# A two-layer hybrid trunk on one core: a reordered chain between sub-layers, and triangular inverses with compact blocks transposed on TensorE

## The chip, the core and the metric

The kernel runs on one core of a Trainium2 chip. Times are device microseconds (us) of that core. The engines are named as the profile names them: PE is TensorE (matmul; PEld is its weight load), DVE is VectorE, ACT is ScalarE, POOL is GpSimd, SP is SyncE, which issues the weight DMAs. Each engine works through its own instructions in order.

## The reference

Two layers, each a token mixer and then a convolutional feed-forward block. Around every one of the four sub-layers stands the same pattern: a modulated RMSNorm in front, a gated RMSNorm behind, and the residual add.

```python
for layer in range(DEPTH):
    mod_p = adaln(c_ctx[None, :], mod_w[layer], mod_b[layer])      # six vectors of 1024
    mod_s = adaln(c, mod_w[layer], mod_b[layer])
    hs = modulated_rmsnorm(xs, n_mix_pre[layer], mod_s[:, 0], mod_s[:, 1])
    ...                                                            # mixer of hp and hs gives op, os_
    xs = xs + mod_s[:, 2, None, :] * rmsnorm(os_, n_mix_post[layer])
    hs = modulated_rmsnorm(xs, n_ffn_pre[layer], mod_s[:, 3], mod_s[:, 4])
    xs = xs + mod_s[:, 5, None, :] * rmsnorm(conv_ffn(hs, *ffn[layer]), n_ffn_post[layer])
def modulated_rmsnorm(x, w, shift, scale):
    return rmsnorm(x, w) * (1.0 + scale[:, None, :]) + shift[:, None, :]
def gated_delta_scan(q, k, v, g, beta, s0):                        # chunks of 128, both directions
    ia = a_strict + jnp.eye(CHUNK)                                 # unit lower triangular, per head
    u = lax.linalg.triangular_solve(ia, vc * bc[..., None], left_side=True, lower=True)
    w = lax.linalg.triangular_solve(ia, kbeta * jnp.exp(gcs)[..., None], left_side=True, lower=True)
```

The prompt has 128 tokens and the sample 256; d_model is 1024 and the feed-forward width 2816. Layer 0 mixes with SSD heads and gated DeltaNet heads, layer 1 with spatial-gating MLP groups and windowed attention.

## The kernel before

All tokens lie side by side in T = 386 columns (128 prompt, 2 of gap, 256 sample), features on the 128 partitions, so the residual stream `xres` is 8 tiles of 128x386. Every dense product is made in three matmuls of split operands (weight high times input high, weight high times input low, weight low times input high): in `acc` (L378 to L380) tile by tile, and in `group` (L393, L395) k by k over up to three output tiles at once. A weight tile comes by one DMA into a `wst` buffer (`fetch`), is cast on ACT (`whi`, L345) and subtracted on DVE (`wlo`, L348). A Tile scheduler fixes the order on each engine by priorities and estimated costs; `tc.issue_after` adds an edge to it.

`Net.residual` is the chain between two sub-layers, run four times: gap 0 (mixer 0 to feed-forward 0), gap 1 (feed-forward 0 to mixer 1), gap 2 (mixer 1 to feed-forward 1), and the last. It needs the sums of squares of the sub-layer's output, of the gated output, and of gated output times x. Tiles 0 to 6 add theirs into `sums` on DVE and POOL (L520). In the middle of tile 7 the callback `before` puts the first of the sums through `colsum` on PE (L498, three 128x1 matmuls for each); behind tile 7 come the other sums and the parts of tile 7 (squares L526, L508; product L530). The root is an add on DVE (L409) and a power on POOL (L412); `spread` sends it back to all partitions on PE (L420); four short DVE instructions (L544 to L411) make the second root's argument. Then `update` forms u on DVE (L563) and adds it to x on POOL (L564), `prenorms` multiplies by the second root (L471), modulates on ACT (L473) in two segments (prompt, sample) and splits into `hh` (ACT, L371) and `hl` (DVE, L372), on which the next matmuls wait.

Beside this runs the adaLN work of the layer as side work in quads: `quads` loads four `wmod` tiles and runs 16 pairs of short matmuls in each of four steps (`pmod`, L301; the profile records a quad as 64), copies the result on ACT (L305), transposes it on PE (L308) and adds the bias on DVE (L310). `step(n)` advances it by n steps; S0, S1 and S2 say how many steps each gap takes behind the first spread, behind the second, and behind each k of `prenorms`; Q0 to Q5 say how many steps other stages take.

The DeltaNet heads need the inverse of a unit triangular 128x128 matrix for each of 8 heads, in 3 chunks. The inverse is built from blocks: 16x16 by scalar recursion on DVE (L887, L889), then 32, 64 and 128 wide by `square` on PE (L922 and L967 to L976). Two matrices PF and PB of 128x8x128 hold the blocks of both directions; the blocks needed as left operands are transposed on DVE (L944 into L2, 4 of 32x256 a chunk, and L962 into L3, 8 a chunk).

## Time and profile before

| what | value |
|---|---|
| median of 3 runs | 1449.47 us (1449.01 to 1450.84) |
| profiled execution, its own time | 1449.51 us |
| its span, mean granted clock of PE | 1447.7 us, 0.975 |
| PE busy | 1379.6 us, 95% of the span |
| DVE, ACT, POOL busy | 956.8, 792.7, 198.4 us |
| chain that ended last, PE's share | 79% |

The span is the time between the first and the last instruction of the profiled execution; its own time has 1.8 us more around it. The 40 slices of the page show PE at 8 or 9 tenths nearly everywhere, but these average over stages: where PE stands idle is read in the timeline around each gap and in the waits of the stretch with the inverses (140 to 262 us).

### The profile page before, as it was taken

What the parts mean: (1) busy time and instruction counts of PE and PEld (TensorE: products, weight loads), DVE (VectorE), ACT (ScalarE), POOL (GpSimd) and SP (SyncE); (2) the same over time, 40 slices, a digit from 0 to 9 for tenths busy, and PEclk for the clock granted to TensorE, in tenths of its full rate; (3) what the DMA queues carried; (4) which work ended last, traced back from release to release, by engine and by line L of the source; (5) the groups of instructions that cost most, each with busy time, mean ns of one, the idle gap of its engine ahead of it and who ended that gap; (6) DMA issues with size and microseconds to landing.
All of it is one profiled execution on the core that took longest, in us unless ns stands there. A gap on an engine that the chain in (4) does not pass through costs nothing.

```text
span 1447.7 us, 26153 instructions
## 1 busy us (share of the span) xinstructions
PE 1379.6 (95%) x10133; PEld 1306.4 (90%) x10133; DVE 956.8 (66%) x1879; ACT 792.7 (55%) x1749; POOL 198.4 (14%) x186
## 2 busy tenths in 40 slices
PE   5999998999998999999999999999999999999996
PEld 3889887999987789899999998999999899999996
DVE  3586999855989766676666445566567486767432
ACT  3578665668585436555455444544855465555341
POOL 0023110012355304200000113000002300000001
PEclk9999999999999999899999999999999999999998
DMA  9334544412643474545543442544234334343441
GB/s 347 130 101 142 174 138 143 142 42 79 199 161 117 139 238 170 210 154 162 170 134 114 128 126 74 160 146 134 83 117 153 125 117 131 117 131 115 128 126 55
DMA packets 60332, 201.58 MB, mean 139 GB/s; under 512 B 7120, under 2 KB 12000, under 8 KB 60208
## 3 DMA queue, kind: packets, MB, share of 16 engines
q1 hardware_dynamic: 52832, 186.25, 40.1%
q10 hardware_dynamic: 6048, 8.93, 1.7%
q0 software_dynamic: 1328, 4.73, 1.1%
q8 instruction: 80, 1.31, 0.4%
q14 instruction: 44, 0.36, 0.1%
HBM read 191.20 MB, written 8.68 MB: 138 GB/s over the span
## 4 chain that ended last, share of the span: by engine, by line
PE 79%; DVE 11%; issue 3%; ACT 3%; POOL 3%; DMA 1%; POOLq 0%; SPq 0%; ACTq 0%; DVEq 0%
PE mm L393 19%; PE mm L378 11%; PE mm L379 11%; PE mm L380 11%; PE mm L395 9%; PE pmod L301 3%; DVE wlo L348 2%; PE ps L498 1%; DVE t L700 1%; PE ps L1625 1%; PE mmt L1550 1%; PE mmt L1551 1%; PE mmt L1552 1%; DVE er L1133 1%; POOL er L809 1%
## 5 line engine op out<-in xcount | busy, mean ns | idle before, releaser
L348 DVE TENSOR_TENSOR wlo<-wst,whi 128x512 fp32r<-128x512 f32 (+1 forms) x497 | 344.2, 699 | 189.0 <-ACT whi L345 185.0
L345 ACT CAST whi<-wst 128x512 fp32r<-128x512 f32 (+1 forms) x505 | 304.2, 612 | 282.9 <-PE mm L379 151.2
L393 PE MATMUL mm<-hh,whi 128*128 128x386 f32 x728 | 247.7, 340 | 5.8 <-ACT hh L371 4.9
L393 PE MATMUL mm<-hh,wlo 128*128 128x386 f32 x728 | 245.9, 338 | 0.0
L395 PE MATMUL mm<-hl,whi 128*128 128x386 f32 x728 | 239.6, 340 | 0.3
L378 PE MATMUL mm<-hh,whi 128*128 128x386 f32 x552 | 198.0, 359 | 4.7 <-ACT t L1341 2.8
L380 PE MATMUL mm<-hh,wlo 128*128 128x386 f32 x552 | 191.6, 347 | 0.6 <-DVE wlo L348 0.6
L379 PE MATMUL mm<-hl,whi 128*128 128x386 f32 x552 | 191.9, 348 | 0.0
L393 PEld LDWEIGHTS mm<-hh,whi 128*128 128x128 f32 x728 | 137.1, 188 | 8.6 <-ACT hh L371 5.8
L395 PEld LDWEIGHTS mm<-hl,whi 128*128 128x128 f32 x728 | 136.1, 188 | 1.5 <-DVE hl L372 1.4
L393 PEld LDWEIGHTS mm<-hh,wlo 128*128 128x128 f32 x728 | 137.3, 189 | 0.0
L378 PE MATMUL mm<-gh,whi 128*128 128x386 f32 x352 | 119.5, 339 | 0.0
L379 PE MATMUL mm<-gl,whi 128*128 128x386 f32 x352 | 119.2, 339 | 0.0
L380 PE MATMUL mm<-gh,wlo 128*128 128x386 f32 x352 | 118.9, 338 | 0.0
L378 PEld LDWEIGHTS mm<-hh,whi 128*128 128x128 f32 x552 | 107.5, 195 | 11.9 <-issue 6.1
L598 DVE SCALAR_TENSOR_TENSOR t<-mm,vecs,t 128x385 f32<-128x385 f32 x88 | 54.3, 618 | 87.1 <-ACT t L597 87.1
L379 PEld LDWEIGHTS mm<-hl,whi 128*128 128x128 f32 x552 | 107.4, 195 | 0.7 <-issue 0.2
L380 PEld LDWEIGHTS mm<-hh,wlo 128*128 128x128 f32 x552 | 106.5, 193 | 1.0 <-DVE wlo L348 0.9
L700 DVE SCALAR_TENSOR_TENSOR t<-mm,vecs,t 128x384 f32<-128x384 f32 (+1 forms) x152 | 92.7, 613 | 12.3 <-ACT t L694 8.1
L597 ACT ACTIVATE t<-mm,vecs 128x386 f32<-128x386 f32 x88 | 58.9, 674 | 72.4 <-PE mm L395 72.4
L520 POOL TENSOR_TENSOR sums<-sums,t 128x386 f32<-128x386 f32 x36 | 41.5, 1175 | 337.6 <-DVE t L517 281.4
L301 PE MATMUL pmod<-wmod,cond 128*32 128x128 f32 x1536 | 67.2, 297 | 0.3 <-issue 0.3
(423 smaller groups left out, 2589.9 us busy)
## 6 DMA issues: line engine op xcount, KB each, us to landing
wmod<-modw_l SPq DMA_DIRECT2D x96, 512.0 KB, 4.4
wst<-up_l SPq DMA_DIRECT2D x88, 512.0 KB, 3.5
wst<-w SPq DMA_DIRECT2D x56, 512.0 KB, 4.0
wst<-wo SPq DMA_DIRECT2D x32, 512.0 KB, 3.9
wst<-down_l SPq DMA_DIRECT2D x32, 512.0 KB, 3.6
wst<-w1f SPq DMA_DIRECT2D x18, 512.0 KB, 3.6
wst<-down_l SPq DMA_DIRECT2D x16, 384.0 KB, 3.2
wst<-w1t SPq DMA_DIRECT2D x10, 512.0 KB, 3.6
```

What stands on the lines that cost most here:

```text
L301: nc.tensor.matmul(acc[32 * c:32 * c + 32, 0:128], self.cond[:, k, :], w[:, o:o + 128], start=(k == 0), stop=(k == 7), tile_position=(0, 3 ...
L345: self.conv_hi = nc.scalar.copy(out=hi[:, 0:m], in_=st[:, o:o + m])
L348: self.conv_lo = eng.tensor_sub(out=lo[:, 0:m], in0=st[:, o:o + m], in1=hi[:, 0:m].bitcast(F32))
L378: mm(ps, wh, xh, start=start, stop=False)
L379: mm(ps, wh, xl, start=False, stop=False)
L380: return mm(ps, wl, xh, start=False, stop=stop)
L393: mm(ps, w[k // 4][p][:, s], hh[:, k, :], start=(k == 0 and p == 0), stop=False)
L395: mm(ps, w[k // 4][0][:, s], hl[:, k, :], start=False, stop=(k == 7))
L520: (nc.gpsimd if i else v).tensor_add(out=acc[:, i, :], in0=acc[:, i, :], in1=p)
L597: nc.scalar.activation(out=cv, in_=ps, func=AF.Identity, scale=cw(1), bias=self.v(f"ffb_l{l}", n))
L598: stt(out=cv[:, 1:T], in0=ps[:, 0:T - 1], scalar=cw(0), in1=cv[:, 1:T], op0=ALU.mult, op1=ALU.add)
L700: nc.vector.scalar_tensor_tensor(out=o, in0=p, scalar=cw(i), in1=o, op0=ALU.mult, op1=ALU.add)
```

## The change

Three things are changed. In the chain between sub-layers the sums of tiles 0 to 6 (in gap 0 of tiles 0 to 5, with tile 6's parts summed on their own) are all taken inside the last tile; the callback comes at k = 14 instead of 16 in the feed-forward blocks, at 4 instead of 5 in mixer 0, and four k later in mixer 1; the third weight tile is fetched right behind the last tile, half of it converted there and half behind the first k of `prenorms`; the first add to x is made on DVE, and the sample segment of the first k is modulated on DVE. The steps of the adaLN work change place: every gap now takes four (one quad): one behind the last tile, and one between and two behind the two spreads, these three held behind the last `colsum`; before, the constants gave gaps 0, 1 and 2 10, 10 and 6 steps. A quad's copy on ACT now comes with the step behind its fourth. Q2, Q4 and Q5 rise, so that other stages take more. In the inverses PF's and PB's diagonal blocks are first made in compact tiles Pd (128x8x32), their transposes are matmuls with an identity on PE followed by copies on ACT, and Pd is copied into PF on ACT and into PB on POOL.

```diff
-S0, S1, S2 = [1, 2, 2], [9, 8, 4], [0, 0, 0]
+S0, S1, S2 = [1, 1, 1], [2, 2, 2], [1, 1, 1]
...
-            for k in (2 * j, 2 * j + 1):
...
-            if j == 3:
-                s = self.t386()[:, 0:128]
-                nc.scalar.copy(out=s, in_=acc[:, 0:128])
+            with self.follow(self.hold):
...
+                        nc.tensor.matmul(acc[32 * c:32 * c + 32, 0:128], self.cond[:, k, :], w[:, o:o + 128],
+                                         start=(k == 0), stop=(k == 7), tile_position=(0, 32 * c))
             yield 0.45
+        s = self.t386()[:, 0:128]
+        nc.scalar.copy(out=s, in_=acc[:, 0:128])
...
-    def fetch(self, after):
...
         st = self.wst.tile([128, 1024], F32, name="wst", tag="wst")
         nc.sync.dma_start(out=st[:, 0:n], in_=src)
         parts = []
+        self.ready.append((src, parts))
+        self.rest = self.halves(st, n, parts)
+        if halves:
+            next(self.rest)
+        else:
+            drain(self.rest)
+
+    def halves(self, st, n, parts):
+        nc = self.nc
         for o in range(0, n, 512):
             m = min(512, n - o)
             hi, lo = (self.spare(n) or p.tile([128, 512], F32R, name=n, tag=n) for n, p in (("whi", self.whi), ("wlo", self.wlo)))
-            with self.follow(after and after[0]):
-                self.conv_hi = nc.scalar.copy(out=hi[:, 0:m], in_=st[:, o:o + m])
+            self.conv_hi = nc.scalar.copy(out=hi[:, 0:m], in_=st[:, o:o + m])
             eng = nc.gpsimd if o and self.help else nc.vector
-            with self.follow(after and after[1]):
-                self.conv_lo = eng.tensor_sub(out=lo[:, 0:m], in0=st[:, o:o + m], in1=hi[:, 0:m].bitcast(F32))
+            self.conv_lo = eng.tensor_sub(out=lo[:, 0:m], in0=st[:, o:o + m], in1=hi[:, 0:m].bitcast(F32))
             parts.append((hi, lo))
-        self.ready.append((src, parts))
+            yield
...
             if update:
-                update(k)
-            nc.vector.tensor_mul(out=h, in0=self.x[:, k, :], in1=r)
+                with self.follow(first and k > 1 and first.ins):
+                    update(k)
+            with self.follow(first and first.ins):
+                nc.vector.tensor_mul(out=h, in0=self.x[:, k, :], in1=r)
             for s, (b, e) in enumerate(SEGS):
+                if update and k == 0 and s:
+                    first = nc.vector.tensor_scalar(out=h[:, b:e], in0=h[:, b:e], scalar1=a[:, k, s:s + 1],
+                                                    scalar2=m[:, k, 0, s:s + 1], op0=ALU.mult, op1=ALU.add)
+                    continue
                 nc.scalar.activation(out=h[:, b:e], in_=h[:, b:e], func=AF.Identity,
                                      scale=a[:, k, s:s + 1], bias=m[:, k, 0, s:s + 1])
-            self.split(hh[:, k, :], hl[:, k, :], h)
-            if update:
-                self.step(S2[self.gap])
+            cast, cut = self.split(hh[:, k, :], hl[:, k, :], h)
+            if update and k == 0:
+                with self.follow(cast.ins), self.follow(cut.ins):
+                    drain(self.rest)
...
+        direct = self.gap == 0
+
         def before():
-            colsum(0, acc[:, 0, :], True)
-            colsum(0, part[0], False)
+            for i in range(num):
+                colsum(i, acc[:, i, :], i == 0)
+            if direct:
+                colsum(0, part[0], False)
...
-            if n:
-                for i, p in list(enumerate(part))[n // 6:]:
+            if 0 < n < 7 - direct:
+                for i, p in enumerate(part):
                     (nc.gpsimd if i else v).tensor_add(out=acc[:, i, :], in0=acc[:, i, :], in1=p)
...
+        six = part
         o = out_tile(7, before)
+        if not last:
+            self.fetch(1)
+        if direct:
+            colsum(2, six[2], False)
...
             for b, e in SEGS:
                 ox = v.tensor_mul(out=part[2][:, b:e], in0=o[:, b:e], in1=gx[:, b:e])
-            colsum(2, acc[:, 2, :], True)
+            self.step(S0[self.gap])
         colsum(0, part[0], False)
...
         if not last:
-            colsum(1, acc[:, 1, :], True)
+            if direct:
+                colsum(1, six[1], False)
...
-            self.step(S0[self.gap])
+            self.hold = tail.ins
+            self.step(S2[self.gap])
             r2 = self.spread(rt2)
             self.step(S1[self.gap])
-            self.prefetch(3, (sq.ins, self.roots[0]))
+            self.hold = None
...
                 v.tensor_mul(out=u[:, n, :], in0=u[:, n, :], in1=r)
-                eng.tensor_add(out=self.x[:, n, :], in0=self.x[:, n, :], in1=u[:, n, :])
+                (eng if n else v).tensor_add(out=self.x[:, n, :], in0=self.x[:, n, :], in1=u[:, n, :])
...
-                    if mid and k0 + k == 16:
+                    if mid and k0 + k == 14:
                         mid()
...
-Q2 = 1
+Q2 = 2
 Q0 = 0
 Q3 = 8
-Q4 = 10
-Q5 = 15
+Q4 = 11
+Q5 = 21
...
-        L = self.w.tile([128, 8, 32], F32, name="L", tag="t2")
-        v.tensor_scalar_mul(out=L[:, :, 0:16], in0=col(TX, 0), scalar1=me)
-        v.tensor_scalar_mul(out=L[:, :, 16:32], in0=col(TXT, 24), scalar1=mo)
+        LP = self.w.tile([128, 2, 8, 32], F32, name="LP", tag="t2")
+        L = LP[:, 0]
+        nc.scalar.activation(out=L[:, :, 0:16], in_=col(TX, 0), func=AF.Copy, scale=me)
+        nc.scalar.activation(out=L[:, :, 16:32], in_=col(TXT, 24), func=AF.Copy, scale=mo)
         yield 0.0, 3.0
-        for a in range(4):
-            p = slice(32 * a, 32 * a + 32)
-            nc.gpsimd.tensor_tensor(out=PB[p, :, 32 * a:32 * a + 32].rearrange("p h (e c) -> p h e c", e=2),
...
-            for P, i, o in ((PF, TXT, 0),):
-                for e in range(2):
-                    nc.scalar.activation(out=P[p, :, 32 * a + 16 * e:32 * a + 16 * e + 16],
-                                         in_=i[p, :, 16 * e + o:16 * e + o + 8].rearrange("p c h -> p h c"),
-                                         func=AF.Copy, scale=(me, mo)[e][p])
+        Pd = self.w.tile([128, 8, 32], F32, name="Pd", tag="Pd"), LP[:, 1]
+        nc.gpsimd.tensor_tensor(out=Pd[1].rearrange("p h (e c) -> p h e c", e=2),
+                                in0=TX.rearrange("p c (e i) -> p i e c", e=2)[:, 8:16],
+                                in1=net.c("eo", 2).unsqueeze(1).unsqueeze(3).to_broadcast([128, 8, 2, 16]), op=ALU.mult)
+        for e in range(2):
+            nc.scalar.activation(out=Pd[0][:, :, 16 * e:16 * e + 16], in_=col(TXT, 16 * e), func=AF.Copy,
...
+        for d, m, o in ((0, me, 16), (1, mo, 0)):
+            v.scalar_tensor_tensor(out=Pd[d][:, :, o:o + 16], in0=O, scalar=m, in1=Pd[d][:, :, o:o + 16],
+                                   op0=ALU.mult, op1=ALU.add)
+        yield 0.0, 1.0
...
+        M = net.ps()[:, 0:256].rearrange("p (h s) -> p h s", h=8)
+        square(M, lambda a, h: NT[blk(a), h, blk(a ^ 1)], lambda a, h: Pd[1 - a % 2][blk(a), h, :], True)
+        O = net.ps()[:, 0:256].rearrange("p (h s) -> p h s", h=8)
+        square(O, lambda a, h: Pd[a % 2][blk(a), h, :], lambda a, h: ident[blk(a), blk(a)], False)
+        yield 1.0, 1.0
+        Ms = evac(M, 32)
+        L2 = self.w.tile([128, 8, 32], F32, name="L2", tag="t4")
+        nc.scalar.copy(out=L2, in_=O)
         for a in range(4):
-            p = blk(a)
-            for P, m, o in ((PF, me, 32 * a + 16), (PB, mo, 32 * a)):
-                v.scalar_tensor_tensor(out=P[p, :, o:o + 16], in0=O[p], scalar=m[p], in1=P[p, :, o:o + 16],
-                                       op0=ALU.mult, op1=ALU.add)
-        L2 = self.w.tile([128, 8, 32], F32, name="L2", tag="t2")
-        for a in range(4):
-            v.transpose(out=L2[blk(a)], in_=(PF, PB)[a % 2][blk(a), :, blk(a)])
-        yield 0.0, 3.0
-        M = net.ps()[:, 0:256].rearrange("p (h s) -> p h s", h=8)
-        square(M, lambda a, h: NT[blk(a), h, blk(a ^ 1)], lambda a, h: (PB, PF)[a % 2][blk(a), h, blk(a)], True)
...
-        Ms = evac(M, 32)
+            for d, P in enumerate((PF, PB)):
+                (nc.gpsimd.tensor_copy if d else nc.scalar.copy)(out=P[blk(a), :, blk(a)], in_=Pd[d][blk(a)])
...
-        L3 = self.w.tile([128, 8, 64], F32, name="L", tag="t3")
...
-                v.transpose(out=L3[o:o + 32, :, (a % 2) * 32:(a % 2) * 32 + 32], in_=P[p, :, o:o + 32])
-        yield 0.0, 3.5
+        yield 0.0, 3.0
+        tr = net.ps()
+        for h in range(8):
+            for a, P in enumerate((PF, PB)):
+                p = slice(64 * a, 64 * a + 64)
+                mm(tr[p, 64 * h:64 * h + 64], P[p, h, p], ident[p, p], start=True, stop=True,
+                   tile_position=(64 * a, 64 * a))
...
-        yield 1.7, 1.5
+        L3 = self.w.tile([128, 8, 64], F32, name="L3", tag="t3")
+        nc.scalar.copy(out=L3.rearrange("p h s -> p (h s)"), in_=tr)
+        yield 2.4, 2.0
...
-                if mid and k == 5:
+                if mid and k == 4:
                     mid()
...
+                w = net.wload(src(n, i))
+                half(ps, w, i, *x, range(4))
                 if mid and i:
                     mid()
-                half(ps, net.wload(src(n, i)), i, *x)
+                half(ps, w, i, *x, range(4, 8))
...
```

PE in gap 0, before: the callback in the last tile (tiles `ps`; `sums` are the accumulated sums, `t_...` a part of one tile, `yh`, `yl` the split mixer output) and the first instructions behind the tile.

```order
L380 MATMUL ps<-yh,wlo 128x386
L498 MATMUL ps<-cst,sums 128x1 x3
L498 MATMUL ps<-cst,t_6492 128x1 x3
L378 MATMUL ps<-yh,whi 128x386
L379 MATMUL ps<-yl,whi 128x386
L380 MATMUL ps<-yh,wlo 128x386
```

The same place in the changed kernel.

```order
L387 MATMUL ps<-yh,wlo 128x386
L513 MATMUL ps<-cst,sums 128x1 x9
L513 MATMUL ps<-cst,t_6639 128x1 x3
L385 MATMUL ps<-yh,whi 128x386
L386 MATMUL ps<-yl,whi 128x386
L387 MATMUL ps<-yh,wlo 128x386
```

All nine column sums and one part of tile 6 now stand ahead of the last four k, and the two remaining parts of tile 6 and those of tile 7 follow the tile.

PE in gap 1, before: from behind the last tile of feed-forward 0 to its second spread of a root (`ps<-cst,rsq`).

```order
L380 MATMUL mm<-gh,wlo 128x386
L498 MATMUL ps<-cst,sums 128x1 x3
L301 MATMUL pmod<-wmod,cond 32x128 x7
L498 MATMUL ps<-cst,t_9559 128x1 x3
L301 MATMUL pmod<-wmod,cond 32x128 x21
L498 MATMUL ps<-cst,sums 128x1 x3
L498 MATMUL ps<-cst,t_9561 128x1 x3
L498 MATMUL ps<-cst,t_9560 128x1 x3
L420 MATMUL ps<-cst,rsq 128x130
L420 MATMUL ps<-cst,rsq 128x128 x2
L301 MATMUL pmod<-wmod,cond 32x128 x5
```

The same place in the changed kernel, on to the first matmul of the next stage (`mm<-hh,whi`).

```order
L302 MATMUL pmod<-wmod,cond 32x128 x8
L513 MATMUL ps<-cst,t_9720 128x1 x3
L513 MATMUL ps<-cst,t_9722 128x1 x3
L513 MATMUL ps<-cst,t_9721 128x1 x3
L302 MATMUL pmod<-wmod,cond 32x128
L427 MATMUL ps<-cst,rsq 128x130
L427 MATMUL ps<-cst,rsq 128x128 x2
L302 MATMUL pmod<-wmod,cond 32x128 x7
L427 MATMUL ps<-cst,rsq 128x130
L427 MATMUL ps<-cst,rsq 128x128 x2
L302 MATMUL pmod<-wmod,cond 32x128 x16
L400 MATMUL mm<-hh,whi 128x386
```

Two sums of `sums` have gone from behind the tile, the `pmod` matmuls behind it went from 7, 21, 5 and 31 to 8, 8 and 16 (of these rows, each stands for two records of the trace), and no bias transpose (L308) is left between the spread and the first matmul.

DVE in gap 1, before, from the last short instruction ahead of the second root to the second product with it.

```order
L411 SCALAR_TENSOR_TENSOR rsq<-q,xx 128x3
L348 TENSOR_TENSOR wlo<-wst,whi 128x512
L548 TENSOR_TENSOR xx<-xx,q 128x3
L348 TENSOR_TENSOR wlo<-wst,whi 128x512
L563 TENSOR_TENSOR u<-u,ps 128x386
L310 TENSOR_TENSOR mod_85<-pmod,vecs 128x8
L563 TENSOR_TENSOR u<-u,ps 128x386 x3
L471 TENSOR_TENSOR t_9710<-xres,ps 128x386
L310 TENSOR_TENSOR mod_85<-pmod,vecs 128x8
L471 TENSOR_TENSOR t_9718<-xres,ps 128x386
```

The same place in the changed kernel, to the low half of the first k.

```order
L418 SCALAR_TENSOR_TENSOR rsq<-q,xx 128x3
L573 TENSOR_TENSOR xx<-xx,q 128x3
L589 TENSOR_TENSOR u<-u,ps 128x386 x2
L590 TENSOR_TENSOR xres<-xres,u 128x386
L481 TENSOR_TENSOR t_9806<-xres,ps 128x386
L484 TENSOR_SCALAR t_9806<-t_9806,ma,mod_85 128x256
L481 TENSOR_TENSOR t_9818<-xres,ps 128x386
L589 TENSOR_TENSOR u<-u,ps 128x386
L379 TENSOR_TENSOR hl<-t_9806,hh 128x386
```

The two `wlo` and the two `mod` (which wait for `pmod`) no longer stand ahead of the products, and an add to `xres` and a modulation have come in.

## Rows read from the trace of the kernel before

**Rows 1.** The page, part 4: the chain that ended last, by engine.

```profile
PE 79%; DVE 11%; issue 3%; ACT 3%; POOL 3%; DMA 1%; POOLq 0%; SPq 0%; ACTq 0%; DVEq 0%
```

**Rows 2.** Busy time by stretch: PE, PEld, DVE, ACT, POOL, granted clock, DMA share, GB/s.

```profile
228.00:240.00 12.00, 8.53 (x151) 7.24 (x152) 11.71 (x26) 7.89 (x22) 3.05 (x4) 0.72 0.11 33
...
574.00:590.00 16.00, 16.00 (x135) 13.51 (x138) 3.90 (x14) 3.04 (x8) 3.59 (x5) 0.51 0.41 145
```

**Rows 3.** Timeline of PE, gap 0: start, us, engine, line, operands, [idle <-releaser].

```profile
571.22 0.83 PE L498 MATMUL ps<-cst,t 128*128 128x1 f32 x6 [1.19 <-ACT t L513]
...
573.74 0.52 PE L379 MATMUL ps<-yl,whi 128*128 128x386 f32 x1
574.06 0.53 PE L380 MATMUL ps<-yh,wlo 128*128 128x386 f32 x1
...
593.75 0.45 PE L393 MATMUL mm<-hh,whi 128*128 128x386 f32 x1 [1.65 <-ACT hh L371]
```

**Rows 4.** Timeline of POOL ahead of gap 0.

```profile
568.30 2.70 POOL L520 TENSOR_TENSOR sums<-sums,t 128x386 f32<-128x386 f32 x2 [0.32 <-ACT t L516]
```

**Rows 5.** Timeline of PE, gap 1.

```profile
883.64 0.34 PE L379 MATMUL mm<-gl,whi 128*128 128x386 f32 x1
883.82 0.34 PE L380 MATMUL mm<-gh,wlo 128*128 128x386 f32 x1
...
885.22 0.83 PE L498 MATMUL ps<-cst,t 128*128 128x1 f32 x6
...
891.80 1.65 PE L420 MATMUL ps<-cst,rsq 128*128 128x130 f32 x6 [0.29 <-POOL rsq L412]
...
897.86 0.44 PE L393 MATMUL mm<-hh,whi 128*128 128x386 f32 x1 [1.65 <-ACT hh L371]
```

**Rows 6.** Timeline of DVE, gap 1.

```profile
889.68 0.16 DVE L544 TENSOR_TENSOR q<-ps,rsq 128x3 f32<-128x3 f32 x1 [3.44 <-PE ps L498]
...
893.66 0.17 DVE L310 TENSOR_TENSOR mod<-pmod,vecs 128x8 f32<-128x8 f32 x1 [1.49 <-PE pmod L308]
...
895.14 0.55 DVE L471 TENSOR_TENSOR t<-xres,ps 128x386 f32<-128x386 f32 x1
```

**Rows 7.** Timeline of ACT, gap 1.

```profile
885.25 1.15 ACT L345 CAST whi<-wst 128x512 fp32r<-128x512 f32 x2
...
895.79 1.61 ACT L473 ACTIVATE t<-t,mod,ma 128x128 f32<-128x128 f32 x3
897.31 0.50 ACT L371 CAST hh<-t 128x386 fp32r<-128x386 f32 x1
```

**Rows 8.** Timeline of POOL, gap 1.

```profile
886.32 0.86 POOL L412 TENSOR_TENSOR rsq<-rsq,mhalf 128x3 f32<-128x3 f32 x1 [11.24 <-DVE rsq L409]
890.50 1.24 POOL L412 TENSOR_TENSOR rsq<-rsq,mhalf 128x3 f32<-128x3 f32 x1 [3.33 <-DVE rsq L411]
```

**Rows 9.** Timeline of PE, gap 2.

```profile
1136.62 0.34 PE L380 MATMUL mm<-mh,wlo 128*128 128x386 f32 x1
...
1150.83 0.45 PE L393 MATMUL mm<-hh,whi 128*128 128x386 f32 x1 [1.64 <-ACT hh L371]
```

**Rows 10.** Timeline of PE: one quad of adaLN work in feed-forward 0.

```profile
606.99 1.96 PE L301 MATMUL pmod<-wmod,cond 128*32 128x128 f32 x64
```

**Rows 11.** Waits of PE, 172 to 260 us: total us, times, longest.

```profile
PE ps L922 <- DVE NR L869: 4.3, 2, 3.6
PE ps L852 <- DVE N L847: 3.1, 2, 2.4
...
PE ps L922 <- ACT PB L980: 0.3, 1, 0.3
```

**Rows 12.** Groups of instructions, 140 to 262 us: busy us, mean ns | idle before.

```profile
L962 DVE STREAM_TRANSPOSE L<-PB 32x256 f32<-32x256 f32 x12 | 5.3, 439 | 0.2
...
L970 ACT COPY Ms<-ps 128x512 f32<-128x512 f32 x3 | 1.8, 595 | 0.5 <-PE ps L968 0.4
```

**Rows 13.** Timeline of PE: one `square` over 4 blocks and 8 heads.

```profile
207.65 0.75 PE L922 MATMUL ps<-Ms,L 32*32 32x32 f32 x64
```

More of the change, by code (lines that the diff above doesn't have):

```diff
@@ L325, in plan @@
     def plan(self, seq):
-        self.seq, self.ready, self.help, self.gap = list(seq), [], False, -1
+        self.seq, self.ready, self.help, self.gap, self.hold = list(seq), [], False, -1, None
         self.more = {"whi": 0, "wlo": 0}
@@ L358, in follow, with prefetch @@
         return self.tc.issue_after(ins) if ins else nullcontext()
-    def prefetch(self, n, after=None):
+    def prefetch(self, n):
         while len(self.ready) < n and self.seq:
-            self.fetch(after)
+            self.fetch()
     def wload(self, src, ahead=2):
@@ L460, in prenorms @@
         step = 8 if mods is None else 2
+        first = None
         for k in range(8):
```

23 lines of the change are left out of this document (8 added, 15 removed).

## The prediction

> **What bounds the kernel now.** I read the chain that ended last first: PE holds 79% of it [rows 1]. So the time is PE's own work plus the places where PE stands or runs slowly. The table by stretch and the timeline show two kinds of such places. The first are the three gaps between sub-layers: from the last matmul of a sub-layer to the first of the next PE passes 574.06 to 593.75 in gap 0 [rows 3], 883.82 to 897.86 in gap 1 [rows 5], 1136.62 to 1150.83 in gap 2 [rows 9], about 19.7, 14.0 and 14.2 us; in gap 0 PE counts as busy all through but at a granted clock of 0.51, its lower level of 1.2 GHz [rows 2]. The second is the stretch with the triangular inverses, where DVE is busy 11.71 of 12 us and PE 8.53 at a granted clock of 0.72 [rows 2], and PE's waits there are for DVE [rows 11]. Everything else the change touches is hidden or is PE work.
>
> I make the sum against the profiled execution, 1449.5 us (span 1447.7 and 1.8 around it); the median of the runs is the same to 0.1 us.
>
> **Gap 1, the simplest.** Before, the chain is stretched by what stands in the queues. PE makes 28 rows of adaLN work (7 and 21 in the order) ahead of and between its sums, so the second root's argument starts only at 889.68 though the first power is done at 887.18 [rows 6, 8]; DVE then waits 1.49 us for a bias transpose of PE before it may go on to the update [rows 6]. After, the order shows only one step of adaLN work ahead of the sums of tile 7, two column sums fewer behind the tile, and no bias step on DVE ahead of the first product. What remains from the end of the last matmul (884.16) is a chain of single instructions: square 0.50 (as the cast of 128x386, [rows 7]), column sum 0.83 [rows 5], add 0.16 [rows 6], power 0.86 [rows 8], four short DVE steps at about 0.2, 0.8 [rows 6], power 1.24 [rows 8], second spread 1.65 [rows 5], product 0.55 [rows 6], modulation of one segment 0.54 (1.61 for three), cast 0.50 [rows 7]. That is 7.6; ten hand-overs at under 0.1 make 8.4; and the first half of the fetched weight tile, a cast of 0.57 that now stands in ACT's queue near the squares [rows 7], may push it: I take 8.8. The update of u and the add to x of the first k, now both on DVE, lie beside the second power and spread, so they cost nothing; without that cover they would be two instructions of 0.55. First matmul at 893.0 instead of 897.86: a gain of 4.9, between 4.3 (every hand-over at 0.15) and 5.5 (no push, and the spread at full clock).
>
> **Gap 2** has the same chain: 1136.96 + 8.8 = 1145.8 against 1150.83 [rows 9], a gain of 5.0, between 4.4 and 5.6.
>
> **Gap 0** differs in its last tile. There the callback now wants all sums of tiles 0 to 5, and the last two adds of these end on POOL at 571.00 [rows 4]; before, PE waited 1.19 us, until 571.22, for a square [rows 3]. So the stall grows by about 1 us, since the callback also comes one k earlier, and behind it stand 18 + 6 records of sums, of which some 1.9 us fall behind 571.0, and twelve matmuls. These start 0.18 us apart at the full clock [rows 5] and 0.32 apart at the lower one [rows 3]: 2.2 to 3.8 us. The tile then ends at 575.1 to 576.7 instead of 574.6. Then the chain of 8.8, or up to 10.4 where each PE step of it runs at the lower clock: first matmul at 583.9 to 587.1 against 593.75. The gain is 6.7 to 9.9; I take 8.0, nearer to the lower clock, which this gap shows in [rows 2].
>
> **The restart.** PE now idles through much of each gap, as its adaLN filler is halved. No row shows the first matmuls of a stage behind such a gap. At full clock from the start they cost nothing; if the clock is at the lower level for the first nine to fourteen of them, each costs 0.14 more (0.32 against 0.18, [rows 3, 5]), 1.3 to 2 us a gap. DVE has a second half of a weight tile, an update and a product for each k beside nine matmuls of 0.18, which is 1.6 us against three instructions of 0.55, so it can hold PE up by some tenths too. I take 1.0 a gap, 3.0 in all, between 0 and 6.0.
>
> **The moved adaLN work.** Before, 384 records stand in the three gaps, after 192. The other 192 are three quads of 1.96 us [rows 10], which go to stages where PE is the bound: a cost of 6.0, and 4.0 at the least, if some of it fills waits of other stages.
>
> **The last residual** loses six of twelve column-sum records in its last tile, of the kind that takes 0.83 for six [rows 5]: a gain of 0.6, since they overlap at the ends.
>
> **The inverses.** DVE loses its 36 transposes of 0.44, 15.8 us in a stretch of 122 [rows 12], and most of the partial adds into PF and PB, which become two full ones a chunk; ACT takes two small scalings and copies instead. PE gains 32 matmuls of 32x32 (64 records) and 16 of 64x64 (32 records) a chunk. One `square` of 64 records takes 0.75 us [rows 13]; taking the 64x64 group as no dearer than 0.9 it is 1.6 a chunk, 4.8 in all. PE's waits for DVE are 4.3 (NR) and 3.1 (N) [rows 11]: with DVE freed I let the first go and half of the second, 5.8. Around 228 to 240 the clock is 0.72 of full over 12 us [rows 2]: 3.4 more if PE is kept fed. 5.8 + 3.4 - 4.8 = 4.4; the new copies on ACT and POOL at the end of a chunk, where little other PE work is left, take back some, so I put 4.0, between -5.0 (only PE's added work counts) and +8.0 (both waits and all of the clock).
>
> Here a rule speaks against the change. DVE's transpose of 32x256 takes 439 ns and four of them make L2 [rows 12], 1.76 us; the matmuls with an identity take at most 0.75 [rows 13], to which an evacuation of 0.595 at most comes [rows 12]. The Trainium skill (VectorE: DVE Perf Modes, section "Rules for kernel authors") says that for a 32x32 transpose within a bank DVE's is fastest. By that rule the term is the -5.0 above and the sum 9 us later. The trace disagrees as to the four instructions in a row, since each handles only 32 partitions, and DVE is the full engine here.
>
> **Sum.** 8.0 + 4.9 + 5.0 - 3.0 - 6.0 + 0.6 + 4.0 = 13.5, so 1449.5 - 13.5 = **1436.0 us**. All terms at their good ends give 25.6 and 1423.9, all at their bad ends a loss of 1.2 and 1450.7.
>
> **Rivals.** *Slow restart.* The clock stays at the lower level for 27 matmuls of each next stage (three k): 27 x 0.14 = 3.8 a gap, 11.4 in place of 3.0, which gives 1444.4. For it: the clock in gap 0 is low for 16 us under weak work [rows 2]. Against it: in gap 1 the matmuls behind the gap already last 0.34 again after the first [rows 5].
>
> *PE's transposes aren't paid back.* PE still waits for NR and N, because other DVE work moves into the freed places; the inverse term is -5.0 and the time 1445.0. For it: DVE is full, with conversions behind. Against it: NR's two waits are the ones right behind the partial adds.
>
> *Everything feeds.* The inverse term is +8.0, the gaps end at full clock and the restart costs 1: 1423.9 to 1430, say 1428.
>
> *The sums find no effect.* Both of the bad cases together, 1444.4 + 9.0 = 1453.4, less 2 for adaLN work that fills waits: 1451, within the noise.
>
> *Slower: ACT's queue in the inverses.* Each chunk now passes ACT at five points in series (Ms, L2 with the copies into PF, the cross blocks, L3, Ms again). If each waits behind two conversions, 1.15 us [rows 7], and ACT's own earlier copies of some 0.6 [rows 12], with nothing for PE to do meanwhile, 15 such points cost 26; the inverse term becomes -22 in place of +4, and the time 1462. It decides from 1.35 us a point on (13.5 + 2.9 + 4.0 = 20.4 over 15). Against it: PE waited for ACT there for 0.3 us in all [rows 11], and ACT is busy 7.89 of 12 us [rows 2].
>
> **Chances.** Forecast (1430 to 1441) 0.52; slow restart 0.14; PE's transposes not paid back 0.10; everything feeds 0.11; no effect 0.06; slower 0.07. A measurement of this kernel tells 0.2%, 2.9 us, from no change. The first four are faster, 0.87; same 0.06; slower 0.07. The range 1425 to 1446 leaves out the last two and the best corner, some 2 in 10.
>
> **What would show it.** In the profile after, gap 1 from the last matmul to the first of mixer 1 should be 9 us or under (over 11 fells the step), with no wait of DVE for `pmod` ahead of the first product; gap 0's tile should show a wait of about 2 us ahead of `sums`, then a gap of 9 to 11. The first matmuls of each stage show by their duration (0.34 or 0.53) what the restart costs. In the inverses PE's wait for NR should be gone and DVE no longer full; waits for ACT's L2, L3 and Ms or POOL's PB of over 1 us would be the slower rival. PE's busy time should rise by some 5 us for the transposes and not change for the adaLN records.

## The result and the profile after

The changed kernel takes 1460.88 us (median of 4 runs, 1457.92 to 1464.22), a ratio of 1.0086 to the kernel before, with a 95% interval of 1.0066 to 1.0105. Timed again beside later experiments it gave 1460.64 us and 1.0085 (1.0054 to 1.0116). The change is slower by about 12 us where 13.5 us of gain were forecast.

The profiled execution (span 1456.1 us) does not show it at first sight. PE is as much of the chain as before, and each gap is shorter. Page, part 4, and busy time by stretch, columns as in [rows 2], the changed kernel; the last fence is the kernel before, in the first group behind gap 0:

```profile
PE 81%; DVE 8%; issue 3%; ACT 3%; DMA 3%; POOL 2%; SPq 0%; POOLq 0%; ACTq 0%; DVEq 0%
```

```profile
228.00:240.00 12.00, 11.15 (x404) 9.64 (x395) 5.96 (x12) 7.27 (x28) 1.82 (x5) 1.00 0.27 81
581.00:594.00 13.00, 12.50 (x107) 10.95 (x106) 4.18 (x14) 2.44 (x7) 3.03 (x4) 0.56 0.22 72
...
594.00:610.00 16.00, 13.18 (x63) 10.74 (x64) 14.41 (x25) 12.39 (x26) 6.95 (x6) 1.00 0.37 113
...
905.24:921.00 15.76, 13.48 (x67) 11.14 (x68) 12.74 (x23) 11.16 (x24) 7.00 (x8) 1.00 0.21 69
...
1159.62:1173.00 13.38, 11.13 (x53) 8.76 (x54) 11.82 (x22) 10.26 (x23) 6.92 (x6) 1.00 0.13 41
```

```profile
593.75:604.80 11.05, 10.94 (x61) 10.62 (x62) 9.65 (x18) 10.06 (x23) 4.92 (x4) 1.00 0.29 117
```

The first row answers to the row of 228 to 240 us in [rows 2]: PE 11.15 instead of 8.53 us of 12, full clock, DVE half idle. In this stretch the inverses did what was wanted. The third row is new trouble: in the 16 us *behind* gap 0 PE is busy 13.18 us only, at full clock, with DVE at 14.41, where the kernel before had PE busy for 10.94 of 11.05 us. The two rows behind it show the same behind gaps 1 and 2. The timeline of PE shows both, the shorter gaps and what follows them (the changed kernel; last matmul of a stage, column sums behind gap 0's tile, first matmul of the next stage, and waits in the first group of feed-forward 0):

```profile
576.39 0.83 PE L513 MATMUL ps<-cst,sums 128*128 128x1 f32 x6 [0.58 <-POOL sums L539]
...
580.68 0.52 PE L387 MATMUL ps<-yh,wlo 128*128 128x386 f32 x1
581.00 1.27 PE L513 MATMUL ps<-cst,t 128*128 128x1 f32 x6
...
583.21 1.44 PE L513 MATMUL ps<-cst,t 128*128 128x1 f32 x6
584.90 4.00 PE L513 MATMUL ps<-cst,t 128*128 128x1 f32 x18 [0.25 <-DVE rsq L416]
...
594.46 0.44 PE L400 MATMUL mm<-hh,whi 128*128 128x386 f32 x1 [0.71 <-ACT hh L378]
...
600.59 0.79 PE L402 MATMUL mm<-hl,whi 128*128 128x386 f32 x3 [0.55 <-DVE hl L379]
...
607.82 0.79 PE L402 MATMUL mm<-hl,whi 128*128 128x386 f32 x3 [0.61 <-DVE hl L379]
...
613.41 0.33 PE L308 MATMUL pmod<-cst,t 128*128 128x128 f32 x1 [1.65 <-ACT t L306]
614.43 0.44 PE L400 MATMUL mm<-hh,whi 128*128 128x386 f32 x1 [0.70 <-DVE t L626]
...
895.19 0.34 PE L387 MATMUL mm<-gh,wlo 128*128 128x386 f32 x1
...
905.24 0.44 PE L400 MATMUL mm<-hh,whi 128*128 128x386 f32 x1 [0.77 <-ACT hh L378]
...
1150.37 0.34 PE L387 MATMUL mm<-mh,wlo 128*128 128x386 f32 x1
...
1159.62 0.44 PE L400 MATMUL mm<-hh,whi 128*128 128x386 f32 x1 [0.22 <-ACT hh L378]
```

From last to first matmul pass 13.8, 10.1 and 9.3 us, against 19.7, 14.0 and 14.2 in [rows 3, 5, 9]. The waits of PE over the whole execution name what came in (engine, line, waited for: total us, times, longest), first the changed kernel, then one row of the kernel before:

```profile
PE pmod L308 <- ACT t L306: 6.7, 5, 3.8
...
PE mm L402 <- DVE hl L379: 4.2, 9, 0.6
PE mm L400 <- ACT hh L378: 4.1, 9, 0.8
...
PE ps L878 <- DVE N L873: 1.4, 1, 1.4
```

```profile
PE pmod L308 <- ACT t L305: 2.7, 5, 1.1
```

To see where time goes, each dense matmul of one trace was paired with the same matmul of the other (the n-th of each kind), and the start in the kernel before taken from the start in the other. A rising number is a loss in that stretch, a falling one a gain. The first column is the changed kernel. The others are experiments that are told below: the kernel before with one part of the change, the changed kernel with two things undone, and the kernel before with two parts (worked out from the timelines; one execution each):

```
start in the    changed   quads    quads,     first   half   inverses  two      half fetch,
kernel before                      old copy   tile    fetch            undone   inverses
 262 inverses      +0.1    -0.2     +0.1      +0.5    -0.2    -4.3     -5.0     -2.6
 478               -1.7    +2.4     +2.3      +0.5    +0.4    -2.0     -5.0     -2.6
 566 mixer 0       +5.4   +10.0     +6.9      +0.5    +1.9    -0.4     -0.3     -2.6
 594 gap 0         +0.7    +5.3     +1.1       0.0    -2.1    -0.2     -6.4     -6.7
 612 first group   +4.6    +7.2     -1.1      +6.0    -0.9    -0.2     -8.4     -5.5
 788 ffn 0         +10.7   +13.9    +4.6      +6.3    -0.9    -1.0     -2.7     -6.3
 898 gap 1         +7.4   +11.3     +3.8      +6.1    -2.0    -1.2     -6.2     -6.5
 908 first group   +11.2   +12.7    +4.7     +10.5    -2.2    -1.2     -4.9     -6.8
1130 mixer 1       +13.1   +16.1    +8.0      +8.7    -3.8    -0.2     -1.9     -8.5
1163 gap 2, group  +10.6   +13.2    +5.6      +7.8    -5.9    -0.4     -5.3    -10.8
1425               +8.7   +11.4     +5.6      +6.0    -7.8    -0.4     -7.2    -12.7
```

In the changed kernel gap 0 gives 4.7 and its first group takes 3.9 back; gap 1 gives 3.3 from 788 on and its group takes 3.8 back by 908. By the same pairing, from the first matmul to the last of the group, the three first groups lose 4.0, 4.1 and 1.8. Mixer 0 from 478 on costs 7.1, and the rest of feed-forward 0 6.1. These are the two losses to explain: the first groups, and the stages that took in adaLN work.

### The profile page after: what moved, and what is told of

Same layout as the page of the kernel before. It is cut to its first block, busy times and chain, and to the rows that moved or that the text cites. A ratio compares the mean times of both kernels' runs of the same rounds, so it can differ in the third digit from the quotient of the medians.

```text
span 1456.1 us, 26672 instructions
## 1 busy us (share of the span) xinstructions
PE 1382.6 (95%) x10415; PEld 1299.4 (89%) x10415; DVE 935.1 (64%) x1828; ACT 793.7 (55%) x1752; POOL 191.6 (13%) x184
## 4 chain that ended last, share of the span: by engine, by line
PE 81%; DVE 8%; issue 3%; ACT 3%; DMA 3%; POOL 2%; SPq 0%; POOLq 0%; ACTq 0%; DVEq 0%
PE mm L400 18%; PE mm L385 12%; PE mm L386 11%; PE mm L387 11%; PE mm L402 9%; PE pmod L302 3%; DVE wlo L355 1%; PE ps L513 1%; PE ps L1652 1%; PE ps L844 1%; PE mmt L1577 1%; PE mmt L1578 1%; PE mmt L1579 1%; POOL er L835 1%; DMA wst<-wo 1%
## 5 line engine op out<-in xcount | busy, mean ns | idle before, releaser
L355 DVE TENSOR_TENSOR wlo<-wst,whi 128x512 fp32r<-128x512 f32 (+1 forms) x497 | 347.7, 705 | 221.1 <-ACT whi L353 217.0
L726 DVE SCALAR_TENSOR_TENSOR t<-mm,vecs,t 128x384 f32<-128x384 f32 (+1 forms) x152 | 92.7, 613 | 16.4 <-ACT t L720 12.8
L385 PEld LDWEIGHTS mm<-gh,whi 128*128 128x128 f32 x352 | 66.5, 189 | 0.0
```

The source lines that it names most:

```text
L355: self.conv_lo = eng.tensor_sub(out=lo[:, 0:m], in0=st[:, o:o + m], in1=hi[:, 0:m].bitcast(F32))
L385: mm(ps, wh, xh, start=start, stop=False)
L726: nc.vector.scalar_tensor_tensor(out=o, in0=p, scalar=cw(i), in1=o, op0=ALU.mult, op1=ALU.add)
```

## The experiments

Medians and ratios are against the kernel before, run on the same chip (its medians there 1448.3 to 1449.0 us); one profiled execution can lie several us off its median.

**The first four: inverses, and the pace behind the gaps.**

The changed kernel with the old inverses (the code of the kernel before from `L` to `Ms`):

> The changed kernel with the inverses of the kernel before (transposes on DVE, blocks written straight into PF and PB). Theory A (the loss sits in the restart of each stage behind a gap and in the moved adaLN work; the new inverses by themselves move the end of their stretch by only +0.7 us): about 1460 us, within 2 us of the changed kernel. Theory B (the new inverses also reorder the rest of mixer 0, where the two traces drift apart by another 7 us between 482 and 543 us): about 1453 us or less.

1460.07 us, 1.0091 (1.0075 to 1.0108): no difference from the changed kernel, theory A.

The kernel before with the new inverses only:

> The kernel before with only the new inverses. Theory A: 1450 us (1448 to 1452), no difference from the kernel before that can be told. Theory B: 1456 us. The forecast on record, a gain of 4.0 from the inverses, would give 1445 us.

1447.92 us, 1.000 (0.998 to 1.0021): no difference, theory A. But its trace ends the stretch 4.3 us earlier (the column "inverses") and gives that back between 380 and 566 us: in this one execution the gain forecast is there and does not reach the end. In the same stretch PE's wait for NR has gone from 4.3 [rows 11] to 1.5 and that for N from 3.1 to 1.5:

```profile
PE ps L919 <- DVE NR L869: 1.5, 1, 1.5
PE ps L852 <- DVE N L847: 1.5, 1, 1.5
```

The two without the adds to x, for the changed kernel and for the kernel before (there `eng` alone makes the add); `...` stands for operands that stay:

```diff
-                (eng if n else v).tensor_add(out=self.x[:, n, :], ...)
+                if last or n == 0:
+                    (eng if n else v).tensor_add(out=self.x[:, n, :], ...)
```

> The changed kernel without the add of u to x for the tiles k = 1 to 7 in gaps 0, 1 and 2 (six or seven POOL instructions of 1.0 to 1.3 us a gap; the residual of these tiles is left out of the computation). Theory A (the first matmuls of a stage are paced by the eight tiles of the pre-norm through DVE, POOL and ACT, 9.6 us over the three gaps): 1453 us, 5 to 8 us less than the changed kernel. Rival C (PE itself restarts slowly, by its clock or its weights): within 2 us of the changed kernel, 1460 us.

> The kernel before without the same adds. Theory A: in the kernel before PE waits only 0.4 us in the first matmuls, as the tiles were prepared while PE still made adaLN work, so the adds are hidden: 1448 us, at most 2 us less than the kernel before. If it falls by as much as the changed kernel does without them, the pace of the pre-norm is no difference between the two kernels and theory A falls.

1450.12 us (1.001, 0.9993 to 1.0027) and 1445.85 us (0.9978, 0.996 to 0.9997). Without the adds the changed kernel gets 10.5 us shorter and the kernel before 2.5. So theory A: behind the gaps the changed kernel waits for the pace of the eight tiles, and the kernel before hardly does. The trace agrees: without the adds the three first groups of the changed kernel cost 0.9, 0.9 and -1.3 instead of 4.0, 4.1 and 1.8. What sets that pace was still open.

**Three on the changed kernel: quads and the first tile.**

```diff
         first = self.group([self.t[f"up_l{l}"][n] for n in range(3)], hh, hl)
+        if not last:
+            self.step(5)
```

> The changed kernel with Q2 = 1 again (one quad of adaLN work less in mixer 0) and five steps placed right behind the first group of feed-forward 0, where the kernel before had a quad of 1.96 us that moved nothing (PE has to wait there for DVE's first results out of PSUM anyway) and the changed kernel waits 2.3 us; Q5 = 22. Theory A (each step that went from a gap into a stage bounded by PE costs 0.65 to 0.75 us, and the quad behind the group was free): the quad less in mixer 0 gives back 3, the four free steps up to 2: 1456 us, 1454 to 1458. Rival D (the 7 us in mixer 0 come from another order of its other work, and the quads fill waits): within 2 us of the changed kernel, 1460 us.

1456.37 us, 1.0045 (1.0026 to 1.0064): 4.3 less, in size as theory A has it.

> The changed kernel with the adaLN schedule of the kernel before (S0, S1, S2, Q2, Q4, Q5, the place of the steps and of the copy as they were), so that each gap holds two quads again; the rest of the change stays. Theory A: the 12 to 15 us that the moved quads cost in mixer 0, feed-forward 0 and mixer 1 come back, and the quads lie in waits that PE has anyway in the gap and in the first group behind it: 1447 us (1444 to 1450). Rival E (the shorter gaps of the changed kernel come from the quads that left them, so the two go together): the gaps lengthen by what the stages win, 1457 to 1460 us.

1450.93 us, 1.0009 (0.9984 to 1.0034): 9.7 less. Rival E falls, and much of the loss hangs on the adaLN schedule. This kernel also issued the copy in its old place, which I took for a detail.

```diff
-                (eng if n else v).tensor_add(...)
+                eng.tensor_add(...)
-                if update and k == 0 and s:
+                if False:
```

> The changed kernel with the first add to x on POOL and the first sample segment modulated on ACT, as before. Theory A (what counts is when the eighth tile of the pre-norm is done, not the first): the first matmul behind each gap comes 0.5 to 1 us later and the eighth tile at the same time: 1460 us, within 2 us of the changed kernel. If the first tile set the end, 2 us more.

1454.99 us, 1.0041 (1.0024 to 1.0058): 5.7 less, where I expected nothing. The edit does more than I had seen: without `first` the later updates are no longer held behind the first tile. In its trace the three first groups cost 1.1, 1.3 and -0.3.

**One part of the change alone, on the kernel before.**

> The kernel before with only the new adaLN schedule (S0, S1, S2, Q2, Q4, Q5, the steps' places in the gap, the hold, the copy behind the fourth step). Theory F (the moved quads cost 13 to 15 us in mixer 0, feed-forward 0 and mixer 1, and buy 7 in gap 0 and 2 to 3 in the others): 1454 us, half of the loss. Rival G (the quads only pay off or cost together with the reordered chain; alone they pay for themselves): 1449 us.

1458.11 us, 1.0072 (1.0045 to 1.0099): +9.5, most of the loss.

> The kernel before with only the new order around the first tile of the pre-norm: the third weight tile fetched in two halves behind the last tile, the first add to x and the first sample segment on DVE, the other tiles held behind them. Theory F (DVE paces the eight tiles, and this gives it a half weight tile, an add and a modulation more among them and holds the updates of the others back): 1453 us, 3 to 5 us slower than the kernel before. Rival H (the loss in the gaps comes from the sums taken inside the last tile): 1449 us.

1452.76 us, 1.0033 (1.0016 to 1.005): +4.2, theory F.

> The kernel before with only the sums of all three kinds taken inside the last tile, the callback at its new places, and in gap 0 tile 6 summed on its own. Theory F: gap 0's last tile waits about 1 us longer for POOL, a few column sums less stand behind each tile, with no effect on the pace behind: 1449 us, within 1.5 us of the kernel before. Rival H: 1453 us or more.

1451.60 us, 1.0017 (0.9998 to 1.0036): within the noise; its profiled execution, 1446.95 us, was 2.6 us shorter than that of the kernel before. Whether it costs a little stays open.

**What in the quads.** Two undo one piece each of the quads-alone kernel: Q2 = 1, and the copy.

> The kernel before with the new adaLN schedule but Q2 = 1, so that mixer 0 keeps its old number of quads and the quad that is left over is made in gap 1. Theory F1 (the quad in mixer 0 costs far more than its 2.6 us of matmuls, because it displaces the fill that covers the waits of its scans; the trace of the schedule alone has mixer 0 end 10 us later): 1449 to 1451 us, 8 us less than with Q2 = 2. Rival F2 (each quad costs its matmuls wherever it stands): 1455 us, 2.6 us less.

1457.51 us, 1.0068 (1.0046 to 1.009). F1 falls, and F2's 1455 lies at the lower end of the interval. In the trace mixer 0 does end some 6 us earlier, but the quad left over is then made in gap 1 and costs there: from 882 to the end of gap 1's first group this kernel loses 3.5 us where the one with Q2 = 2 gains 1.1.

```diff
+            if j == 3:
+                s = self.t386()[:, 0:128]
+                nc.scalar.copy(out=s, in_=acc[:, 0:128])
             yield 0.45
-        s = self.t386()[:, 0:128]
-        nc.scalar.copy(out=s, in_=acc[:, 0:128])
```

> The kernel before with the new adaLN schedule but the copy of a quad's result issued with its fourth step, as before. Theory F1: the place of the copy does not matter, 1458 us. Rival F3 (with the copy a step later each quad holds its accumulator longer and so delays other tiles in all the stages with quads): 1453 us or less.

1451.31 us, 1.0026 (1.001 to 1.0043): 6.8 less than with the late copy. F3 holds. The end of the first group of feed-forward 0 shows how, in quads alone, PE and then ACT:

```profile
614.86 0.33 PE L308 MATMUL pmod<-cst,t 128*128 128x128 f32 x1 [1.65 <-ACT t L306]
615.88 0.44 PE L393 MATMUL mm<-hh,whi 128*128 128x386 f32 x1 [0.70 <-DVE t L601]
```

```profile
612.89 0.62 ACT L345 CAST whi<-wst 128x512 fp32r<-128x512 f32 x1 [1.29 <-PE mm L395]
613.42 1.23 ACT L598 ACTIVATE t<-mm,vecs 128x386 f32<-128x386 f32 x2
614.54 0.26 ACT L306 COPY t<-pmod 128x128 f32<-128x128 f32 x1
```

The accumulator of gap 0's quad was finished in the gap, but its copy now belongs to the next step, and there it stands on ACT behind a cast and two results of the group. PE's transpose waits 1.65 us for it with everything behind it in order. The second wait has another cause: the pool `pmm` has four PSUM buffers, three hold the group and the fourth still holds the quad, so the fourth tile waits for DVE to empty one (L601 reads the group's first tile). The kernel before had at this place a quad of 1.96 us that held the fourth buffer too [rows 10], and a wait:

```profile
609.83 0.42 PE L393 MATMUL mm<-hh,whi 128*128 128x386 f32 x1 [0.88 <-DVE t L600]
```

With the old copy the fourth buffer is free and the trace has neither wait: the row "first group" of that column falls by 2.2 instead of rising by 1.9. The waits of PE for this copy, with the old place:

```profile
PE pmod L309 <- ACT t L306: 2.1, 5, 0.4
```

That is 2.1 us against 4.3 with the late copy in the same kernel, and 6.7 in the changed kernel. The largest of those falls in the inverses:

```profile
194.19 0.47 PE L308 MATMUL pmod<-cst,t 128*128 128x128 f32 x1 [3.77 <-ACT t L306]
```

There it eats what the inverses win: from 180 to 195 us the changed kernel goes from -2.3 to +2.0 against the kernel before, where "inverses" alone stays at -1.8 and -1.6; at 262 the two have +0.1 and -4.3.

**What in the first tile.** The half fetch alone, and the whole part without the hold:

> The kernel before with only the third weight tile fetched in two halves behind the last tile; the first add to x, the first sample segment and the order of the updates as before. Theory F (the add and the modulation on DVE and the updates held behind them cost): 1449 us. Rival F4 (the half conversions among the first tiles cost): 1452 to 1453 us, the same as the whole part.

1444.46 us, 0.9978 (0.996 to 0.9996): 4 us *faster* than the kernel before.

```diff
-                with self.follow(first and k > 1 and first.ins):
+                with self.follow(None):
-            with self.follow(first and first.ins):
+            with self.follow(None):
```

> The kernel before with the new order around the first tile (half fetch, first add and first sample segment on DVE), but without the rule that holds the updates and products of the later tiles behind the first tile's modulation. Theory J (the hold costs: three updates that DVE made in its waits for the second root and for the adaLN results now come behind the first tile, and the eighth tile with them): 1445 us, as with the half fetch alone. Rival K (the add and the modulation on DVE cost by themselves): 1451 to 1453 us, as with the whole part.

1444.56 us, 0.997 (0.9956 to 0.9985). Theory J: the add and the modulation on DVE cost nothing, the hold costs about 8 us. The timeline of DVE in gap 0 from the second root's argument on, with the hold and then without:

```profile
585.57 0.16 DVE L561 TENSOR_TENSOR q<-ps,rsq 128x3 f32<-128x3 f32 x1 [6.54 <-PE ps L513]
...
587.54 0.55 DVE L579 TENSOR_TENSOR u<-u,ps 128x386 f32<-128x386 f32 x1
588.00 0.56 DVE L580 TENSOR_TENSOR xres<-xres,u 128x386 f32<-128x386 f32 x1
589.78 0.17 DVE L310 TENSOR_TENSOR mod<-pmod,vecs 128x8 f32<-128x8 f32 x1 [1.23 <-PE pmod L308]
...
592.65 0.17 DVE L310 TENSOR_TENSOR mod<-pmod,vecs 128x8 f32<-128x8 f32 x1 [2.24 <-PE pmod L308]
...
593.52 0.55 DVE L579 TENSOR_TENSOR u<-u,ps 128x386 f32<-128x386 f32 x1
...
594.46 1.52 DVE L355 TENSOR_TENSOR wlo<-wst,whi 128x512 fp32r<-128x512 f32 x1
...
598.52 0.56 DVE L481 TENSOR_TENSOR t<-xres,ps 128x386 f32<-128x386 f32 x1 [0.67 <-POOL xres L580]
...
606.10 0.56 DVE L481 TENSOR_TENSOR t<-xres,ps 128x386 f32<-128x386 f32 x1 [0.91 <-POOL xres L580]
...
608.84 0.55 DVE L379 TENSOR_TENSOR hl<-t,hh 128x386 fp32r<-128x386 f32 x1
```

```profile
583.57 0.16 DVE L561 TENSOR_TENSOR q<-ps,rsq 128x3 f32<-128x3 f32 x1 [3.44 <-PE ps L513]
...
587.21 0.17 DVE L310 TENSOR_TENSOR mod<-pmod,vecs 128x8 f32<-128x8 f32 x1 [1.37 <-PE pmod L308]
587.29 1.95 DVE L579 TENSOR_TENSOR u<-u,ps 128x386 f32<-128x386 f32 x4
...
590.42 0.17 DVE L310 TENSOR_TENSOR mod<-pmod,vecs 128x8 f32<-128x8 f32 x1 [0.72 <-PE pmod L308]
...
592.34 0.68 DVE L355 TENSOR_TENSOR wlo<-wst,whi 128x512 fp32r<-128x512 f32 x1
...
602.06 0.55 DVE L379 TENSOR_TENSOR hl<-t,hh 128x386 fp32r<-128x386 f32 x1
```

The last row of each is the low half of the eighth tile, the last thing that the first group needs. Without the hold DVE makes four updates between its two waits for adaLN results, six in all ahead of the first product, and the second wait shrinks to 0.72 us. With the hold two are made ahead, DVE stands idle 2.24 us in the second wait with updates at hand, and makes six later, among the tiles, where two products wait 0.67 and 0.91 us for POOL's adds (without the hold one waits, 0.45) and a subtraction beside such an add takes 1.52. The eighth tile is ready at 609.4 instead of 602.6.

Not all of these 6.8 us is the hold. The second root's argument already comes 2.0 us earlier in the execution without it, and PE's granted clock there over 575 to 592 us was 0.81 against 0.55, the first row with the hold:

```profile
575.00:592.00 17.00, 16.85 (x172) 14.53 (x171) 4.14 (x14) 2.15 (x7) 3.03 (x4) 0.55 0.39 129
```

```profile
575.00:592.00 17.00, 14.76 (x183) 13.07 (x183) 8.59 (x24) 5.08 (x14) 8.83 (x10) 0.81 0.62 209
```

The pairing from the first matmul of each group to its last leaves this out: the three groups cost 4.6, 4.3 and 2.0 us with the hold and 0.6, 0.2 and 0.2 without it. The changed kernel has 4.0, 4.1 and 1.8. An early first matmul is worth nothing by itself here, as all three tiles of the group need the eighth.

**All together.** First the changed kernel with the copy in its old place and without hold, add and modulation on DVE for the first tile; then two candidates on the kernel before:

> The changed kernel with two things undone: the copy of a quad's result is issued with its fourth step again, and the first add, the first sample segment and the order of the updates are as before. If the parts add up (half fetch -4, moved quads with the old copy +2.9, inverses 0, sums 0 to +3): 1447 to 1450 us, 11 to 14 less than the changed kernel. If the shortened gaps need the first tile on DVE, 1455 us.

1447.95 us, 0.9983 (0.9965 to 1.0001): 12.7 less than the changed kernel. Undoing these two gives back the whole loss; what is left of the change takes as long as the kernel before.

> The kernel before with the new inverses and the sums inside the last tile, and nothing else of the change; the candidate for a version better than both. If the profiled executions tell right (the inverses alone end their stretch 4.3 us earlier and give it back in mixer 0; the sums alone end 2.1 us earlier): 1446 us. If the timed runs tell right (1447.9 and 1451.6): 1450 us.

1449.18 us, 1.0004 (0.9988 to 1.0019): no gain from these two parts.

> The kernel before with the half fetch and the new inverses, and nothing else of the change: the candidate for a version better than both. 1444 us (1442 to 1446), if the inverses go on giving back in mixer 0 what they win; 1441 us if their 4 us survive here.

1441.35 us, 0.9957 (0.9935 to 0.998): 7 us less than the kernel before and 19 less than the changed one. Against the half fetch alone (0.9978, 0.996 to 0.9996) the rest is within the noise, so whether the inverses win anything here stays open.

## Why the prediction was wrong

**The gaps** were right in direction and, but for gap 0, nearly in size: gaps 1 and 2 from last to first matmul are shorter by 4.0 and 5.0 (4.9 and 5.0 forecast; 4.0 is under the lower end of 4.3). Gap 0's 8.0 (6.7 its lower end) had the longer last tile in it: the tile lost 1.2, about as forecast, with a wait for POOL of 0.58 at 576.39, the gap gave 5.9, and 4.7 is left. Its chain was put at 8.8 to 10.4 and took 13.3, from 581.20 to 594.46. It was taken over from gap 1 with one column sum of 0.83; here 30 records of sums stand behind the tile, those of tile 6 among them, and take 1.27, 1.44 and 4.00 us at a clock of 0.56 over the gap. The last residual gave 0.3 (+8.7 at 1425, +8.4 at the end) of 0.6.

**The restart** failed. I put 1.0 a gap, 3.0 in all and 6.0 at the worst, from matmuls at the lower clock and some tenths for DVE, whose three instructions a tile take as long as PE's nine matmuls. Measured from the first matmul to the last of the group 4.0, 4.1 and 1.8 come back, 9.9 in all, at a granted clock of 1.00 in all three groups. The step missed the hold: the text says that the update and add of the first tile "lie beside the second power and spread, so they cost nothing", and never asks which updates lay there before. The order that stood in front of me shows it (one and then three updates ahead of the first product before, two after). I counted those updates and DVE's wait for adaLN results only as what kept the first product back; the hold moved the updates among the tiles, where DVE is busy for 14.41 of 16 us behind gap 0. The end of the chain was put at the first matmul instead of at the eighth tile.

**The moved adaLN work** failed twice. I had 6.0 for three quads, one each that mixer 0, feed-forward 0 and mixer 1 take in. In the column "quads, old copy", where neither the late copy nor the inverses take part, mixer 0 (478 to 566) loses 4.6 and mixer 1 (908 to 1130) 3.3. Feed-forward 0 behind 612 loses 5.7, but for two quads (256 records in place of 128): one of them stood before in the wait behind the first group, and its going gives 3.0 there (+1.9 at the group's end, -1.1 behind it). That makes 10.6 in all. Why a quad costs more than its 1.96 us of matmuls is not taken apart. In the changed kernel, with the late copy, the same stages lose 7.1, 6.1 and 1.9. And the copy that moved a step on has no term in my sum at all. Undone in quads alone it is worth 6.8 us, in size more than half of the loss. I had read that edit as order without cost, and named neither what the copy queues behind on ACT nor that its accumulator holds one of four PSUM buffers for a step more. With the old copy the whole schedule costs 2.9 us net, as the gaps get shorter (gap 0 by 5.8 in that column).

**The inverses** were right in their stretch (+4.0 forecast, 4.3 in the trace of that part alone) and wrong in the sum: timed alone they change nothing, and in the changed kernel the late copy took them back. The trace says that PE's extra matmuls were paid back in the stretch, as DVE was the engine waited for [rows 11]. The Trainium skill's rule that DVE's transpose is the fastest for 32x32 within a bank (VectorE: DVE Perf Modes, section "Rules for kernel authors") did not decide the stretch here. Why 2.6 to 4.3 us are given back in the rest of mixer 0 in one kernel and kept in the other ("half fetch, inverses") is not settled.

**The half fetch** I counted as a push of 0.4 a gap. Alone it is a gain of 4 us. In its trace the time from the second root's argument to the first matmul falls from 8.7, 8.2 and 8.4 us in the three gaps to 8.6, 7.0 and 6.0. That fits the order of gap 1 before, where two subtractions of the third weight tile stand ahead of the updates; no run takes this apart from the edges on the fetch that the edit drops with it.

**The rivals.** None was the one that came. The slower one named ACT's queue in the inverses, and its time, 1462, came near the measured one by luck: ACT's queue it was, but for one adaLN copy that stood in it (3.77 us in the inverses and 1.65 in feed-forward 0), and not for five points in every chunk. The slow restart came nearly in size, 9.9 of 11.4, and not by its clock. Two sums do not come out as written: the bad ends of the terms add up to a loss of 1.0 and not 1.2, and by the slower rival's own numbers 16.4 over 15 points decide, 1.1 us a point and not 1.35. And the 0.34 behind gap 1 that speaks against the slow restart is in the trace (898.14) but not in [rows 5]. None of this changes the account.

## What to carry to other kernels

Shortening the wait for the first tile of a group is worth what the *last* tile gains: ask when the last input of the group is ready, and what the engine made in the waits that are removed. A copy that frees a shared buffer and that an in-order engine waits for should be issued where its input is ready, not a step later. Take a change of several parts apart before judging it: here one part won 4 us, and two small edits cost three times as much.

## What the runs showed of the hardware

The subtraction of a half weight tile on DVE took 1.52 us beside an add on POOL (the row at 594.46 above, 0.96 us of it beside this add) and 0.68 us without it (592.34), both with two SBUF inputs.

```profile
594.15 1.27 POOL L580 TENSOR_TENSOR xres<-xres,u 128x386 f32<-128x386 f32 x1 [4.68 <-DVE u L579]
```

In the same execution the 449 subtractions of weight tiles that had nothing on POOL beside them took at most 0.70 us. The Trainium skill (GPSIMD Engine Reference, section "1. Specifications") says that POOL shares its SBUF interfaces with VectorE and contends with instructions that have two SBUF inputs; the rows agree.

The up projection of feed-forward 1 (1163 to 1344 us) ran 1.8 to 1.9 us faster in some profiled executions than in that of the kernel before, evenly along the stretch, with the same instructions on PE. The changed kernel did so in one profiled execution and not in the other, so it is part of the scatter of single executions. No run tells why.
